# mLSTM, retention and SSD units: a chunk's final transposes share a step with the scores of the chunk three further on

## The chip, the cores and the metric

The kernel runs on one core of one Trainium2 chip. The metric is the device time of one launch in microseconds (us), lower is better; it is given as a median of runs. Every step of the argument is read from one profiled execution. Engines are named as the profile names them: PE (TensorE), PEld (its weight loads), DVE (VectorE), ACT (ScalarE), POOL (GpSimd), SP (DMA issue).

## The reference, cut to what matters

One inference step of a two-layer encoder. A projection W_in is split among four branches, each a causal recurrence done chunk by chunk; the gated results are concatenated and go through W_out. The change touches three branches:

```python
hn = rmsnorm(x, norm_w)
proj = jnp.einsum("btd,dc->btc", hn, w_in)
...
# mLSTM, retention, SSD, each per chunk: scores, output, state
s = jnp.einsum("bhlk,bhsk->bhls", q, k) * dec
o = (jnp.einsum("bhls,bhsv->bhlv", s, v)
     + jnp.exp((idx[None] + 1.0) * lg[:, None])[..., None] * jnp.einsum("bhlk,bhkv->bhlv", q, s_prev))
s_new = jnp.exp(l * lg)[:, None, None] * s_prev + jnp.einsum("bhsk,bhsv->bhkv", kw, v)
...
out_r = head_layernorm(from_blocks(hr)).reshape(bsz, t, GROUP_WIDTH) * jax.nn.silu(rg)
...
y = x + jnp.einsum("btc,cd->btd", jnp.concatenate([out_m, out_r, out_s, out_h], axis=-1), w_out)
```

The prompt has 1024 frames; eight running streams bring 16 frames each.

## The kernel before

The 1152 frames are nine chunks of 128 (eight of the prompt, the ninth the eight streams). Each layer has ten units, two mLSTM (`m`), two retention (`r`), two SSD (`s`) and four HGRN2 (`h`), in the order h r s m h r s m h h. A unit has a projection (its columns of W_in, float32 split into high and low parts: L404 to L406 and L425 to L427, three matmuls for each tile of the contraction) and a mix (the recurrence).

A unit's mix is issued while the next unit's projection runs: r's mix beside s's projection, s's beside m's, m's beside h's. `merge` interleaves the two. A mix is a generator that yields after each step and names its number of steps; after each half of a projection tile `merge` takes as many steps as keep the two in proportion (`j * np_ * pace < i * nm_`, with `nm_` the number of steps). An `after(lag, fn)` puts work off by that many steps. SSD's projection also carries a convolution on DVE (the taps at L1176, the clamp of a SiLU at L526, its sigmoids on ACT at L215, the transposes of its tail on PE at L1200, a product on POOL), tied to projection tiles, not to mix steps. The weights' split into `hi` (ACT, L202) and `lo` (DVE or POOL, L212) is tied to projection tiles too.

A chunk of a mix is made of these parts:

- Z: what the scores need ahead (r: two transposes at L1014 and their copies; m: a copy by head on POOL; s: E prepares the decay).
- A: the scores (r: L1027; m: L812 and L813; s: L1255 and L1258) and their product with the decay on DVE.
- B: the output and the new state (r: L1042, L1043, L1050; m: L841 onwards; s: L1289 onwards). In r, DVE then adds the chunk's product to the state `rS` (L212), scales it (L1059), takes means and variances of the output tile `po` (L1080, L1081), waits for ACT's reciprocal root (L215), normalises (L1085, the last to read `po`) and multiplies by the gate (L212).
- C: two transposes of the gated result on PE (r: L1095, m: L912, s: L1350), a copy out of PSUM, and after two chunks a DMA to `mixd`.

All PSUM tiles (`w` in the trace) come from one pool of eight buffers, whatever asks for them; a projection tile and the parts of a mix draw from it in program order:

```python
self.p_tr = pool("tr", 8, space=PSUM)
```

The step order of r was

```python
A(c); Z(c + 2); yield
B(c - 1); yield
Cc(c - 2); yield
```

and those of m and s the same three steps with E(c + 1) ahead of C. In s, the copies after A and the state update after B were put off with `after(LAG, ...)`.

Of the kernel before, what the change touches and what calls it, by code (L numbers as in the profile page):

```python
# [35 lines left out]
LAG = 1  # L36
# [12 lines left out]
NCH = 9  # L49
# [71 lines left out]
class Kernel:  # L121
    def __init__(self, nc, tc, ctx, T):
        self.nc, self.tc, self.T = nc, tc, T
        pool = lambda name, bufs, **k: ctx.enter_context(tc.tile_pool(name=name, bufs=bufs, **k))
        self.p_const = pool("const", 1)
        self.p_big = pool("big", 6)
        self.p_hi = pool("whi", 2)
        self.p_lo = pool("wlo", 2)
        self.p_raw = pool("wraw", 4)
        self.p_f = pool("f", 18)  # L130
        self.p_c = pool("c", 21)
        self.p_t = pool("t", 8)
        self.p_lay = pool("lay", 1)
        self.p_st = pool("st", 1)
        self.p_s = pool("s", 6)
        self.p_bl = pool("bl", 7)
        self.p_dram = pool("dram", 1, space=DRAM)
        self.p_tr = pool("tr", 8, space=PSUM)
        self.n = 0
        self.ticks = 0  # L140
        self.queue = []
        self.steps = 0
        self.after_queue = []
        self.rest = ((), 0)
# [566 lines left out]
    def unit_m(self, l, p):  # L711
# [38 lines left out]
        def mix():  # L750
# [9 lines left out]
            def Z(c):  # L760
                g, o = divmod(c * 128, G3)
                qz[c] = self.by_head(q[g][:, o:o + 128])
# [167 lines left out]
            use_wi(0)  # L930
            E(0)
            yield
            for c in range(NCH + 1):
                if c % 2 == 0 and c // 2 + 1 < 5:
                    load_e(c // 2 + 1)
                if c % 3 == W1 and c // 3 + 1 < 3:
                    load_wi(c // 3 + 1)
                if c % 3 == W2 and c // 3 + 1 < 3:
                    use_wi(c // 3 + 1)
                if c == 5:  # L940
                    load_states()
                if c < NCH:
                    A(c)
                    if c + 1 < NCH:
                        Z(c + 1)
                    yield
                if c >= 1:
                    B(c - 1)
                    yield
                if c + 1 < NCH:  # L950
                    E(c + 1)
                if c >= 2:
                    Cc(c - 2)
                    yield
            yield
            Cc(NCH - 1)
            yield

        return dict(runs=[("tm", ev_v), ("tm", ev_o), ("tm", ev_z), ("fm", ev_qk)], mix=mix, steps=29, gate=None)


    def unit_r(self, l, p):
# [35 lines left out]
        def mix():  # L998
# [10 lines left out]
            def Z(c):  # L1009

                j, i = divmod(c, 2)
                tr = self.ps("tr")
                for a in range(2):
                    nc.tensor.transpose(tr[:, 128 * a:128 * a + 128], qk[j][:, 256 * i + 128 * a:256 * i + 128 * a + 128], self.ident)  # L1014
                t = self.f()
                self.tt(t[:, 0:256].rearrange("p (h t) -> p h t", h=2), tr[:, None, 0:128].to_broadcast([128, 2, 128]),
                        self.HM[:, :, None].to_broadcast([128, 2, 128]), ALU.mult)
                self.copy(t[:, 256:384], tr[:, 128:256], "a")
                qkT[c] = t
                if c == 8:  # L1020
                    U["zq"] = [self.zq(t[:, 128 * h:128 * h + 128], slice(64 * h, 64 * h + 64)) for h in range(2)]
                    U["km"] = self.km(qk[j][:, 256 * i + 128:256 * i + 256], "c")
# [84 lines left out]
            for c in range(NCH + 1):  # L1107
                if c == 5:
                    load_states()
                if c < NCH:  # L1110
                    A(c)
                    if c + 2 < NCH:
                        Z(c + 2)
                    yield
                if c >= 1:
                    B(c - 1)
                    yield
                if c >= 2:
                    Cc(c - 2)
                    yield  # L1120
            Cc(NCH - 1)
            yield

        return dict(runs=[("tm", ev_qk), ("tm", ev_v), ("tm", ev_g)], mix=mix, steps=29, gate=None)


    def unit_s(self, l, u):
# [96 lines left out]
        def mix():  # L1224
# [26 lines left out]
            def A(c):  # L1251
                g, o = divmod(c * 128, G3)
                cs = slice(o, o + 128)
                sc = self.ps("sc")
                nc.tensor.matmul(sc[:, 0:128], post[2, g][:, cs], post[3, g][:, cs], start=True, stop=True)  # L1255
                tr = sc[:, 128:512]
                for a in range(3):
                    nc.tensor.transpose(tr[:, 128 * a:128 * a + 128], post[a, g][:, cs], self.ident)  # L1258
                e = eb.pop(c)
                Pt[c] = e  # L1260
                xx = self.c(512)
                x, cb_b = self.t(256), self.t(256)
                cb, b_ = cb_b[:, 0:128], cb_b[:, 128:256]
                xd[c], xw[c], xs[c], bt[c] = xx[:, 0:256], xx[:, 256:512], x, b_

                def evac():
                    self.tt(cb, sc[:, 0:128], self.U[c == 8], ALU.mult)
                    self.tt(v4(xx[:, 0:256]), v4(tr[:, 0:256]), sc4(0, c), ALU.mult)
                    self.copy(x, tr[:, 0:256], "a")
                    self.copy(b_, tr[:, 256:384], "a")  # L1270
                    self.tt(e, cb[:, None, :].to_broadcast([128, 4, 128]), e, ALU.mult, "p")
                    self.tt(v4(xx[:, 256:512]), v4(xx[:, 0:256]), sc4(3, c), ALU.mult, "p")
                    self.tt(v4(x), v4(x), self.dsk[:, l, 4 * u:4 * u + 4][:, :, None].to_broadcast([128, 4, 64]), ALU.mult, "p")
                    if c == 8:
                        U["zq"] = self.zq(post[3, g][:, cs])
                        U["km"] = self.km(b_, "c")

                self.after(LAG, evac)

            def B(c):  # L1280
                j, i = divmod(c, 2)
# [13 lines left out]
                if c < 8:  # L1295
                    tr = self.ps("tr")
                    nc.tensor.matmul(tr[:, 0:256], b_, w_, start=True, stop=True)

                    def update():
                        if c == 0:  # L1300
                            self.copy(H, tr[:, 0:256], "v")
                        else:
                            self.tt(v4(H), v4(H), sc4(4, c), ALU.mult)
                            self.tt(H, H, tr[:, 0:256], ALU.add)
                        if c == 7:
                            self.dma(T["o_p_s"][l, 4 * u:4 * u + 4].rearrange("h k v -> k h v"), v4(H))

                    self.after(LAG, update)
                else:
                    km = U.pop("km")  # L1310
                    for jj in range(4):
                        tr = self.ps("tr")
                        for n in range(2):
                            nn = 2 * jj + n
                            nc.tensor.matmul(tr[:, 256 * n:256 * n + 256], km[nn], w_, start=True, stop=True)
                        s = stt[jj]
                        for n in range(2):
                            d = self.sg[:, 5, 8 * (2 * jj + n) + 4 * u:8 * (2 * jj + n) + 4 * u + 4][:, :, None].to_broadcast([128, 4, 64])
                            self.tt(s[:, n], s[:, n], d, ALU.mult, "p")
                        s2 = s.rearrange("p n h e -> p (n h e)")  # L1320
                        self.tt(s2, s2, tr, ALU.add)
                        for n in range(2):
                            self.dma(T["o_s_s"][l, 2 * jj + n, 4 * u:4 * u + 4].rearrange("h k v -> k h v"), s[:, n])
# [48 lines left out]
            for c in range(NCH + 1):  # L1372
                if c + 2 < NCH:
                    load_e(c + 2)
                if c == 5:
                    load_states()
                if c < NCH:
                    A(c)
                    yield
                if c == 0:  # L1380
                    yield
                if c >= 1:
                    B(c - 1)
                    yield
                if c + 1 < NCH:
                    E(c + 1)
                if c >= 2:
                    Cc(c - 2)
                    yield
            yield  # L1390
            yield
            Cc(NCH - 1)
            yield

        return dict(runs=[("fm", ev_x), ("tm", ev_z), ("fm", ev_bc)], mix=mix, steps=33, gate=None)


    def unit_h(self, l, h):
# [602 lines left out]
```

## Time and profile before

| what | before |
|---|---|
| median of 3 runs | 2383.02 us (2382.79 to 2383.59) |
| profiled execution | 2383.27 us |
| its span | 2381.4 us |
| mean granted clock of PE | 0.994 of full |

The span is what the profile covers; 1.9 us of the execution's time lie around it. The profile gives for each engine its busy time, for each stretch of time what was busy in it, and for each wait of an engine which other engine ended it.

### The profile page before, as it was taken

The page shows a single profiled execution, that of the slowest core. Times are in us where ns is not written, and L with a number is a line of the kernel's source. Part 1 is how long each engine was busy: PE and PEld are TensorE (multiplying, and loading weights), DVE is VectorE, ACT ScalarE, POOL GpSimd, SP SyncE. Part 2 cuts the span into 40 slices and gives each one's busy share as a digit, 9 for nine tenths or more (in the row PEclk, how much of TensorE's full clock was granted, in tenths as well). Part 3 has the DMA queues.
Part 4 walks back from the last instruction along what each step waited for, and adds up shares of the span by engine and source line. Part 5 has one row for each costly group of instructions (what it writes and reads, how often), then busy time and mean ns, then how long its engine had stood idle before and what let it go on. Part 6 is the DMA issues. An engine that isn't in the chain of part 4 may idle for free.

```text
span 2381.4 us, 51682 instructions
## 1 busy us (share of the span) xinstructions
PE 2315.6 (97%) x20104; PEld 2251.8 (95%) x20104; DVE 1367.5 (57%) x3426; ACT 1082.4 (45%) x2881; POOL 935.8 (39%) x1117
## 2 busy tenths in 40 slices
PE   7999999999999998999999999999999999899998
PEld 7899999999999998999998999999899999888998
DVE  4756753774765377553258476537747555766532
ACT  6344563433555345424354445634344653453333
POOL 2442344353334335434316333433633452344341
PEclk9999999999999999999999999999999999999999
DMA  5111232221123222546411212322111323225462
GB/s 153 37 47 53 79 90 78 66 61 53 50 84 96 62 73 66 171 126 207 136 49 34 62 55 85 87 70 74 49 54 52 105 72 83 50 86 163 146 189 96
DMA packets 280048, 205.24 MB, mean 86 GB/s; under 512 B 56788, under 2 KB 272236, under 8 KB 279804
## 3 DMA queue, kind: packets, MB, share of 16 engines
q1 hardware_dynamic: 279484, 201.85, 29.9%
q8 instruction: 159, 2.61, 0.5%
q14 instruction: 85, 0.70, 0.1%
q0 software_dynamic: 320, 0.09, 0.0%
HBM read 149.58 MB, written 52.29 MB: 85 GB/s over the span
## 4 chain that ended last, share of the span: by engine, by line
PE 84%; DVE 8%; ACT 4%; DMA 1%; issue 1%; SPq 1%; POOL 1%; ACTq 0%; DVEq 0%; POOLq 0%
PE w L425 16%; PE w L427 16%; PE w L426 16%; PE w L404 6%; PE w L405 6%; PE w L406 6%; DVE f L212 3%; ACT f L215 2%; PE w L1289 1%; DVE c L212 1%; DMA c<-mixd 1%; PE w L1642 1%; PE w L1603 1%; PE w L1552 1%; PE w L1043 1%
## 5 line engine op out<-in xcount | busy, mean ns | idle before, releaser
L425 PE MATMUL w<-hi,hnh 128*128 128x256 f32 (+1 forms) x2592 | 773.3, 298 | 0.0
L427 PE MATMUL w<-hi,hnl 128*128 128x256 f32 (+1 forms) x2592 | 730.1, 282 | 1.6 <-DVE hnl L492 1.4
L426 PE MATMUL w<-lo,hnh 128*128 128x256 f32 (+1 forms) x2592 | 729.3, 281 | 0.0
L425 PEld LDWEIGHTS w<-hi,hnh 128*128 128x128 f32 x2592 | 490.6, 189 | 5.7 <-issue 0.8
L426 PEld LDWEIGHTS w<-lo,hnh 128*128 128x128 f32 x2592 | 490.9, 189 | 2.9
L427 PEld LDWEIGHTS w<-hi,hnl 128*128 128x128 f32 x2592 | 490.3, 189 | 2.2 <-DVE hnl L492 2.0
L215 ACT ACTIVATE f<-f 128x384 f32<-128x384 f32 (+1 forms) x460 | 236.3, 516 | 427.7 <-DVE f L212 263.5
L215 ACT ACTIVATE c<-c 128x512 f32<-128x512 f32 (+3 forms) x398 | 211.3, 534 | 286.3 <-DVE c L526 202.2
L212 POOL TENSOR_TENSOR f<-f,f 128x384 f32<-128x384 f32 (+2 forms) x268 | 225.6, 849 | 290.7 <-ACT f L215 216.3
L404 PE MATMUL w<-hnh,hi 128*128 128x384 f32 x960 | 338.8, 353 | 0.0
L425 PE MATMUL w<-hi,mxh 128*128 128x256 f32 x1152 | 329.4, 286 | 0.0
L427 PE MATMUL w<-hi,mxl 128*128 128x256 f32 x1152 | 325.2, 282 | 0.2 <-POOL mxl L212 0.2
L426 PE MATMUL w<-lo,mxh 128*128 128x256 f32 x1152 | 324.9, 282 | 0.0
L406 PE MATMUL w<-hnh,lo 128*128 128x384 f32 x960 | 324.6, 338 | 0.0
L405 PE MATMUL w<-hnl,hi 128*128 128x384 f32 x960 | 324.6, 338 | 0.0
L212 POOL TENSOR_TENSOR lo<-raw,hi 128x512 fp32r<-128x512 f32 x148 | 196.4, 1327 | 304.3 <-ACT hi L202 278.3
L212 POOL TENSOR_TENSOR c<-c,c 128x512 f32<-128x512 f32 (+2 forms) x144 | 160.3, 1122 | 273.3 <-ACT c L215 169.5
L425 PEld LDWEIGHTS w<-hi,mxh 128*128 128x128 f32 x1152 | 219.0, 190 | 1.4 <-issue 0.6
L427 PEld LDWEIGHTS w<-hi,mxl 128*128 128x128 f32 x1152 | 219.0, 190 | 0.8 <-POOL mxl L212 0.8
L426 PEld LDWEIGHTS w<-lo,mxh 128*128 128x128 f32 x1152 | 218.2, 189 | 0.0
L212 DVE TENSOR_TENSOR lo<-raw,hi 128x512 fp32r<-128x512 f32 x140 | 114.8, 820 | 149.9 <-ACT hi L202 149.7
L404 PEld LDWEIGHTS w<-hnh,hi 128*128 128x128 f32 x960 | 181.5, 189 | 3.0 <-issue 1.8
(295 smaller groups left out, 3876.8 us busy)
## 6 DMA issues: line engine op xcount, KB each, us to landing
raw<-in_w_in SPq DMA_DIRECT2D x224, 128.0 KB
raw<-in_w_in SPq DMA_DIRECT2D x112, 256.0 KB
c<-mixd SPq DMA_DIRECT2D x96, 192.0 KB
raw<-in_w_out SPq DMA_DIRECT2D x64, 256.0 KB
mixd<-c SPq DMA_DIRECT2D x48, 256.0 KB
xd<-c SPq DMA_DIRECT2D x48, 256.0 KB
c<-xd SPq DMA_DIRECT2D x48, 256.0 KB
c<-sscr SPq DMA_DIRECT2D x36, 256.0 KB
```

Source lines behind the costliest of these rows:

```text
L212: (self.nc.vector if e == "v" else self.nc.gpsimd).tensor_tensor(out=out, in0=a, in1=b, op=op)
L215: self.nc.scalar.activation(out=out, in_=in_, func=func, scale=scale, bias=bias, **k)
L404: nc.tensor.matmul(o, hi[:, k, ms], xhi[:, k, :], start=(k == 0), stop=False)
L405: nc.tensor.matmul(o, hi[:, k, ms], xlo[:, k, :], start=False, stop=False)
L406: nc.tensor.matmul(o, lo[:, k, ms], xhi[:, k, :], start=False, stop=(k == KT - 1))
L425: nc.tensor.matmul(o, xhi[:, k, ts], hi[:, k, :w], start=(k == 0), stop=False)
L426: nc.tensor.matmul(o, xhi[:, k, ts], lo[:, k, :w], start=False, stop=False)
L427: nc.tensor.matmul(o, xlo[:, k, ts], hi[:, k, :w], start=False, stop=(k == KT - 1))
L1043: nc.tensor.matmul(po[h], w[:, h], v[j][:, i, h], start=(c in (0, 8)), stop=(c < 8))
L1289: nc.tensor.matmul(po[:, 64 * h:64 * h + 64], pt[:, h], x_[:, 64 * h:64 * h + 64], start=True, stop=True)
L1552: nc.tensor.matmul(sc[rs, 16 * c:16 * c + 16].rearrange("p (n t) -> p n t", t=hs), xt, half(xt), start=True, stop=True)
L1603: nc.tensor.matmul(tr[:, cs], W["KT"][:, cs], v[j][:, i, 0], start=True, stop=True)
```

## The change

A chunk's C is no longer a step of its own. C of chunk c - 3 is issued at the end of the step of A of chunk c (before: C of chunk c - 2, a step behind B of chunk c - 1). r keeps B as a second step; m and s put B of chunk c - 1 and E of chunk c + 1 together in a second step. The last three C are steps of their own at the end. The number of steps falls from 29 to 23 (m, r) and from 33 to 26 (s). In m, Z runs two chunks ahead rather than one. In s, `evac` and `update` are issued at once rather than put off. The pool `t` has 10 buffers, before 8.

```diff
-        self.p_t = pool("t", 8)
+        self.p_t = pool("t", 10)
...
             E(0)
             yield
+            Z(1)
             for c in range(NCH + 1):
...
                     A(c)
-                    if c + 1 < NCH:
-                        Z(c + 1)
+                    if c + 2 < NCH:
+                        Z(c + 2)
+                    if c >= 3:
+                        Cc(c - 3)
                     yield
                 if c >= 1:
                     B(c - 1)
-                    yield
                 if c + 1 < NCH:
                     E(c + 1)
-                if c >= 2:
-                    Cc(c - 2)
-                    yield
+                yield
+            Cc(NCH - 3)
+            yield
+            Cc(NCH - 2)
             yield
             Cc(NCH - 1)
             yield
-        return dict(runs=[("tm", ev_v), ("tm", ev_o), ("tm", ev_z), ("fm", ev_qk)], mix=mix, steps=29, gate=None)
+        return dict(runs=[("tm", ev_v), ("tm", ev_o), ("tm", ev_z), ("fm", ev_qk)], mix=mix, steps=23, gate=None)
...
     def unit_r(self, l, p):
                     A(c)
                     if c + 2 < NCH:
                         Z(c + 2)
+                    if c >= 3:
+                        Cc(c - 3)
                     yield
                 if c >= 1:
                     B(c - 1)
                     yield
-                if c >= 2:
-                    Cc(c - 2)
-                    yield
...
     def unit_s(self, l, u):
-                self.after(LAG, evac)
+                evac()
...
-                    self.after(LAG, update)
+                    update()
...
-        return dict(runs=[("fm", ev_x), ("tm", ev_z), ("fm", ev_bc)], mix=mix, steps=33, gate=None)
+        return dict(runs=[("fm", ev_x), ("tm", ev_z), ("fm", ev_bc)], mix=mix, steps=26, gate=None)
```

In the changed file the lines of `unit_r` are three higher: L1030 for L1027, L1017 for L1014, L1045 for L1042, L1062 for L1059, L1083 and L1084 for L1080 and L1081, L1088 for L1085, L1098 for L1095; the taps are L1182, the tail L1206.

First place: PE, in the mix of the first retention unit, about the scores of the sixth chunk (`w334` before, `w332` after; `f301`, `f304` its query and key, `t310` the gated result of the third chunk whose transposes are C). Before, C stands between projection matmuls, right behind a tail transpose of the convolution:

```order
L426 MATMUL w318_2849<-lo6_2437,hnh21_231 128x256
L427 MATMUL w318_2849<-hi6_2436,hnl22_232 128x256
L1200 MATMUL w324_2919<-cst_107,t293_2677 27x128
L1095 MATMUL w326_2929<-cst_107,t310_2778 128x128 x2
L425 MATMUL w318_2849<-hi6_2436,hnh21_231 128x256
L426 MATMUL w318_2849<-lo6_2437,hnh21_231 128x256
```

After, the same transposes of `t310` follow the scores and Z:

```order
L427 MATMUL w329_2954<-hi6_2430,hnl22_232 128x256
L1030 MATMUL w332_2962<-f304_2750 128x256
L1017 MATMUL w334_2966<-cst_107,c156_1442 128x128 x2
L1098 MATMUL w336_2972<-cst_107,t310_2796 128x128 x2
L425 MATMUL w329_2954<-hi6_2430,hnh21_231 128x256
L426 MATMUL w329_2954<-lo6_2431,hnh21_231 128x256
```

C moved behind A and Z; no instruction of PE is gone. Fewer projection matmuls stand between one B and the next: from B with `w307` to B with `w320` 51 before and 45 after, from there to B with `w340` 51 before and 42 after.

Second place: DVE in the same stretch, from the masking of Z's `w316` to the normalisation of the output tile `w320` of chunk 4. Before, the state update of `rS` comes right after the clamp of a SiLU (L526), and the weight split `lo7` after the gate product:

```order
L212 TENSOR_TENSOR f317_2846<-w316_2843,cst_107 128x256
L526 TENSOR_SCALAR f292_2675<-f292_2675 128x384
L212 TENSOR_TENSOR rS249_2394<-rS249_2394,w321_2879 64x128 x2
L1059 TENSOR_SCALAR rS249_2394<-rS249_2394,cst_107 128x128
L1080 BN_STATS s322_2884<-w320_2874 128x6
L1081 BN_AGGR s322_2884<-s322_2884 128x2
L1080 BN_STATS s322_2884<-w320_2874 128x6
L1081 BN_AGGR s322_2884<-s322_2884 128x2
L1085 TENSOR_SCALAR t323_2891<-w320_2874,s322_2884 128x128 x2
L212 TENSOR_TENSOR t323_2891<-t323_2891,c231_2198 128x256
L212 TENSOR_TENSOR lo7_2809<-raw7_1_2493,hi7_2808 128x2x256
```

After, `lo7` and two taps of the convolution stand ahead of the state update:

```order
L212 TENSOR_TENSOR f317_2848<-w316_2845,cst_107 128x256
L526 TENSOR_SCALAR f288_2654<-f288_2654 128x384
L212 TENSOR_TENSOR lo7_2804<-raw7_1_2493,hi7_2803 128x2x256
L1182 SCALAR_TENSOR_TENSOR f297_2717<-c296_2712,vA_134,f297_2717 128x256
L1182 SCALAR_TENSOR_TENSOR f297_2717<-c296_2712,vA_134,f297_2717 128x128
L212 TENSOR_TENSOR rS249_2394<-rS249_2394,w321_2897 64x128 x2
L1062 TENSOR_SCALAR rS249_2394<-rS249_2394,cst_107 128x128
L1083 BN_STATS s322_2902<-w320_2892 128x6
L1084 BN_AGGR s322_2902<-s322_2902 128x2
L1083 BN_STATS s322_2902<-w320_2892 128x6
L1084 BN_AGGR s322_2902<-s322_2902 128x2
L1088 TENSOR_SCALAR t323_2909<-w320_2892,s322_2902 128x128 x2
```

The split moved ahead of the update. It reads `hi7`, which ACT writes behind the three sigmoids of the SiLU whose clamp is the second row. The buffer of `w320`, which L1088 (before: L1085) is the last to read, goes to the product `w341` of the next chunk's B before, and to that B's output `w340` itself now. The same shifts stand in all four retention units.

Third place: ACT there, from the sigmoids of the gate (`c312`) to the reciprocal root of chunk 4 (`s322`):

```order
L215 ACTIVATE c312_2824<-c312_2824 128x512 x2
L202 ACTIVATE f317_2848<-w316_2845 128x128
L202 ACTIVATE c306_2756<-w318_2851 128x2x128
L215 ACTIVATE f319_2862<-f288_2654 128x384
L215 ACTIVATE f319_2862<-f319_2862 128x384 x2
L202 ACTIVATE hi7_2803<-raw7_1_2493 128x2x256
L215 ACTIVATE s322_2902<-s322_2902,eps_112 128x2
```

Before, the reciprocal root `s322` stood ahead of `hi7`; now `hi7` stands ahead, behind the sigmoids `f319`.

## Rows read from the trace of the kernel before
**Rows 1.** The page: busy time of each engine, and the chain that ended last by engine.

```profile
PE 2315.6 (97%) x20104; PEld 2251.8 (95%) x20104; DVE 1367.5 (57%) x3426; ACT 1082.4 (45%) x2881; POOL 935.8 (39%) x1117
...
PE 84%; DVE 8%; ACT 4%; DMA 1%; issue 1%; SPq 1%; POOL 1%; ACTq 0%; DVEq 0%; POOLq 0%
```

**Rows 2.** Waits of PE: line, what it waited for, us in all, times, longest.

```profile
PE w L1584 <- DVE f L212: 12.0, 8, 2.9
...
PE w L871 <- ACT f L202: 1.7, 2, 0.9
```

**Rows 3.** Windows of the first mixes of r, s, m, and h's start.

```profile
core 0: us, PE busy (x) PEld busy (x) DVE busy (x) ACT busy (x) POOL busy (x), PEclk, DMA share, GB/s
193.00:284.00 91.00, 91.00 (x667) 88.81 (x666) 66.60 (x179) 43.43 (x99) 26.05 (x29) 1.00 0.21 57
291.00:377.00 86.00, 86.00 (x708) 84.14 (x707) 49.31 (x104) 55.11 (x149) 42.83 (x54) 1.00 0.35 92
414.00:481.00 67.00, 67.00 (x510) 64.46 (x509) 48.03 (x158) 29.31 (x111) 21.87 (x29) 1.00 0.26 67
...
505.00:517.00 12.00, 10.06 (x111) 9.60 (x112) 10.82 (x22) 3.48 (x8) 6.97 (x9) 0.86 0.17 45
```

**Rows 4.** Timeline of PE about two C of r: start, us, instructions.

```profile
223.59 0.28 PE L427 MATMUL w<-hi,hnl 128*128 128x256 f32 x1
223.71 0.38 PE L1095 MATMUL w<-cst,t 128*128 128x128 f32 x2
...
224.05 0.27 PE L426 MATMUL w<-lo,hnh 128*128 128x256 f32 x1
...
232.14 0.28 PE L427 MATMUL w<-hi,hnl 128*128 128x256 f32 x1
232.26 0.27 PE L1200 MATMUL w<-cst,t 128*27 128x128 f32 x1
232.37 0.38 PE L1095 MATMUL w<-cst,t 128*128 128x128 f32 x2
...
232.71 0.28 PE L426 MATMUL w<-lo,hnh 128*128 128x256 f32 x1
```

**Rows 5.** Timeline of PE: B of chunks 3, 4 and 5 of r.

```profile
220.62 0.38 PE L1042 MATMUL w<-rS,f 128*128 128x128 f32 x2
...
228.81 0.39 PE L1042 MATMUL w<-rS,f 128*128 128x128 f32 x2
...
237.26 0.38 PE L1042 MATMUL w<-rS,f 128*128 128x128 f32 x2
```

**Rows 6.** Timeline of DVE there; in brackets the idle time before and what ended it.

```profile
222.14 0.58 DVE L212 TENSOR_TENSOR rS<-rS,w 64x128 f32<-64x128 f32 x2 [0.51 <-PE w L1050]
...
225.70 1.77 DVE L1176 SCALAR_TENSOR_TENSOR f<-c,vA,f 128x256 f32<-128x256 f32 x2
...
229.97 0.34 DVE L526 TENSOR_SCALAR f<-f 128x384 f32<-128x384 f32 x1
230.33 0.58 DVE L212 TENSOR_TENSOR rS<-rS,w 64x128 f32<-64x128 f32 x2
...
233.12 0.73 DVE L1085 TENSOR_SCALAR t<-w,s 128x128 f32<-128x128 f32 x2 [0.60 <-ACT s L215]
...
234.23 0.69 DVE L212 TENSOR_TENSOR lo<-raw,hi 128x512 fp32r<-128x512 f32 x1
234.83 0.74 DVE L1176 SCALAR_TENSOR_TENSOR f<-c,vA,f 128x256 f32<-128x256 f32 x2
```

**Rows 7.** Timeline of ACT there: sigmoids of a SiLU, the weights' `hi`.

```profile
230.35 1.64 ACT L215 ACTIVATE f<-f 128x384 f32<-128x384 f32 x3
...
233.00 0.62 ACT L202 ACTIVATE hi<-raw 128x512 fp32r<-128x512 f32 x1
```

**Rows 8.** Timeline of POOL there.

```profile
225.48 1.44 POOL L212 TENSOR_TENSOR lo<-raw,hi 128x512 fp32r<-128x512 f32 x1 [1.09 <-ACT hi L202]
...
232.07 1.01 POOL L212 TENSOR_TENSOR f<-f,f 128x384 f32<-128x384 f32 x1 [0.57 <-ACT f L215]
```

**Rows 9.** Window of a chunk of s in which ACT has most.

```profile
341.00:349.50 8.50, 8.50 (x72) 8.40 (x71) 5.08 (x11) 7.45 (x22) 4.92 (x5) 1.00 0.20 55
```

More of the change, by code (lines that the diff above doesn't have):

```diff
@@ L1117, in mix @@
                     yield
-                if c >= 2:
-                    Cc(c - 2)
-                    yield
+            Cc(NCH - 3)
+            yield
+            Cc(NCH - 2)
+            yield
             Cc(NCH - 1)
             yield
-        return dict(runs=[("tm", ev_qk), ("tm", ev_v), ("tm", ev_g)], mix=mix, steps=29, gate=None)
+        return dict(runs=[("tm", ev_qk), ("tm", ev_v), ("tm", ev_g)], mix=mix, steps=23, gate=None)
     def unit_s(self, l, u):
@@ L1378, in mix @@
                     A(c)
-                    yield
-                if c == 0:
+                    if c >= 3:
+                        Cc(c - 3)
                     yield
@@ L1383, in mix @@
                     B(c - 1)
-                    yield
                 if c + 1 < NCH:
                     E(c + 1)
-                if c >= 2:
-                    Cc(c - 2)
-                    yield
+                yield
+            Cc(NCH - 3)
             yield
+            Cc(NCH - 2)
             yield
```

## The prediction

> **What bounds the kernel now.** I read the page's busy times and chain first, then the waits of PE, then windows of each kind of stage, then the timelines of one retention chunk. The page gives PE 2315.6 us of a span of 2381.4 and 84% of the chain [rows 1], so only two things count: instructions that PE no longer executes, and time in which it waits. In the windows of the first r, s and m mixes PE is busy all of the time at full clock (91.00 of 91.00, 86.00 of 86.00, 67.00 of 67.00 us) [rows 3]: no time waits there to be won. PE idles elsewhere, chiefly where an h unit starts: L1584 alone waits 12.0 us for DVE, and the window of the first such start has 10.06 us of PE in 12.00 at a mean clock of 0.86 [rows 2, 3]. Of the stages that the change touches only L871, the stream part of m, waits: 1.7 us in two waits for an ACT copy [rows 2]. What the change can lose is hidden so far: DVE has 66.60 of 91.00 us in r, ACT 55.11 of 86.00 in s, DVE 48.03 of 67.00 in m [rows 3]. These are means; the steps of a mix come closer together now, so the question is where another engine is full for a whole chunk.
>
> **The merged transposes: 0 us.** 72 of the C that stood alone now stand behind A. A lone C costs PE this: from the L427 before it to the L426 after it 0.46 us (223.59 to 224.05), where two matmuls' spacing takes 0.24 (0.12 from that L427 to where C starts), so 0.22 for the two transposes. Behind a tail transpose the same pair of neighbours is 0.57 apart (232.14 to 232.71), that is 0.33 for three, again 0.11 for each [rows 4]. Standing together saves nothing that these rows show; their rounding of 0.01 us for each C, either way, makes a bound of 0.7 us.
>
> **L871: -1.7 us.** In m the third buffer that the stream part fills was last read by an ACT copy issued a moment before; with another order of requests it gets one that DVE emptied earlier. The wait of 1.7 us goes [rows 2]; bounds 0 (another wait takes its place) and -1.7.
>
> **Denser chunks in r: +7.8 us.** From B of chunk 3 to B of chunk 4 it was 228.81 - 220.62 = 8.19 us, to the next 237.26 - 228.81 = 8.45 [rows 5]. The order has 6 and 9 projection matmuls fewer there; at 0.118 us each (0.24 for two, above) B now come at 0, 7.48 and 14.87 us.
>
> DVE doesn't follow. Count from B of chunk 3. The state add starts 1.52 us after B (222.14 against 220.62), and DVE had been idle 0.51 us for it. The next state add starts at 230.33, 9.71 us after that B, with only a wait for the reciprocal root between (one such wait is 0.60 us): DVE was full and just in time, since 228.81 + 1.52 is the same 230.33 [rows 5, 6]. All this work stands between the two adds after the change as well, so the clamp that came before the add still ends at 230.31 - 220.62 = 9.69. But now the weight split `lo7` comes next. It waits for `hi7`, and that for three sigmoids which themselves wait for the clamp: 1.64 + 0.62 us [rows 7], with the 0.04 and 0.06 us from end to start that these engines show it can begin at about 12.05. The split takes 0.60 (234.23 to 234.83), two taps 0.74 [rows 6]: the state add starts at 13.4, its product ready since 7.48 + 1.52 = 9.0. From the add to the end of L1085 it was 233.12 + 0.73 - 230.33 = 3.52 us [rows 6], so `po` of chunk 4 is free at 16.9. B of chunk 5, due at 14.87, takes this very buffer and stands still for about 1.95 us, all of PE's work behind it. (A tail transpose ahead of it takes the buffer of the state product and stops for part of that; it is the same wait.) In the kernel before, B of chunk 5 didn't need it: only the state product did, and L1085 ended at 233.85, 3.4 us ahead of B at 237.26. Four retention units: 4 x 1.95 = 7.8 us.
>
> Bounds. Low: the two taps at 225.70 took 1.77 us where the two at 234.83 took 0.74; if that 1.03 doesn't recur in the new order, a stall of 0.9 is left. At most another 0.4 may go with single instructions that start earlier than added up: 0.5 each, 2 us in all. High: after the stall B and DVE run in step, the next split again stands ahead of a state add behind its sigmoids, and by the same sums the B after next is late by about 0.5: 2.5 each, 10 us.
>
> POOL's split of 225.48 lasts to 226.92 and ends inside the slow tap, 0.29 us before the end of its first half [rows 6, 8]. The Trainium skill, page "SBUF — State Buffer", section "SBUF: two separate sides", says that VectorE and GpSimd share a pair of ports under an exclusive lock, and that a VectorE instruction with two SBUF inputs is blocked until GpSimd's ends; the slow tap agrees. By this rule the 1.03 comes back, since POOL's split still follows `hi`, and `lo7` would be caught by POOL's product behind the sigmoids (1.01 us, with 0.4 left of it as `lo7` starts): 4 x 2.35 = 9.4 us instead of 7.8, and a time of 2390.7. I keep 7.8, which rests on durations alone.
>
> **Denser chunks in s and m: 0 us.** In s the fullest chunk has ACT 7.45 of 8.50 us [rows 9]. The chunks come about 12% closer, 7.5 us, so ACT is just full there, not over, and the gated result has two steps before its C. If it fails by a chunk's missing slack, up to 1 us in each of four units: bound +4. In m DVE's 48.03 of 67.00 leaves room even 12% denser. Z two chunks ahead takes POOL's copy off A's path, where PE didn't wait. The ten buffers of `t`, and `evac` and `update` at once, cost nothing: the same instructions, issued earlier, hidden under a PE that is full.
>
> **Sum.** 2383.27 (the profiled execution: span 2381.4 and 1.9 around it) + 7.8 - 1.7 + 0 + 0 = 2389.4; the median of the runs is 0.25 lower, so 2389.1, say 2389, +0.25%. Its own bounds: +2 - 1.7 - 0.7 gives 2382.6, +10 + 0.7 + 4 gives 2397.7.
>
> **Rivals.**
>
> - *DVE keeps up (0.35).* If `hi7` isn't late, or the clamp comes earlier since other work of DVE moves behind it, the buffer is free before B is due. The chain has 1.95 us to lose. For it: DVE had 24.4 us of 91.00 free in r [rows 3] and starts the chain on time. Against: the free time lies elsewhere, in this chunk DVE waited only 0.60 us. Then only L871 stays: 2383.0 - 1.7 = 2381.3, with up to 0.4 for each r unit 2383.
> - *Faster (0.13).* The mixes end earlier within their stage, so DVE is free sooner for what h's start waits for. L1584's 12.0 us stand in 8 waits [rows 2]; if half of them were m's mix still in DVE's queue, 6 us go and with them 1.7 of L871: 2375.3, which decides from the point where m's last gate products end before h's first clamp. Against: m's mix is through by 481 and h waits at 505, where DVE's 10.82 us of 12.00 [rows 3] are h's own. A smaller case is that L871 and one or two of these waits go: 2378.
> - *The stall repeats (0.05).* DVE and PE stay in step over three or four chunks of r, or s adds its 4 us: 2398 and above.
> - The forecast itself: 0.47.
>
> **How the numbers follow.** A measurement of this kernel tells about 0.2% (4.8 us) from no change. Slower by more: the forecast but for its low end (a stall below 1.6), 0.42, and the last rival, 0.05: 0.47. Within: DVE keeps up, 0.35, and that low end, 0.05: 0.40. Faster by more: 0.13. Eight in ten leave out the last rival and the larger part of the third: from 2379, the smaller faster case, to 2398. The forecast's own range is 2386 to 2394.
>
> **What the profile would show.** The timeline of the first r mix: a PE idle of 1 to 3 us about 15 us after B of chunk 3 at L1206 and L1045, released by DVE (L212 on `rS`, L1088), in all four units and nowhere else in r; PE's waits gain a line of 4 to 10 us. DVE's split should start right after ACT's `hi`, the state add 4 us after its product. L871 should be gone from the waits; C's transposes should still cost 0.22 us. The prediction is wrong if PE is busy 91 of 91 us in r as before (first rival), if the waits at L1584 shrink (second), or if s or m show a wait at L1289 or L1356.

## The result, and the profile after

The changed kernel takes 2407.56 us in the median (2402.67 to 2409.51, 4 runs) against 2382.9 beside it: a ratio of 1.0101, 95% interval 1.0084 to 1.0119. It is slower by 1.0%; 0.25% was forecast, and the time lies above both stated ranges (2386 to 2394, and 2379 to 2398). The profiled execution took 2405.74 us with a span of 2403.8, 22.4 more than before.

First the page of the changed kernel, busy time of each engine:

```profile
PE 2320.8 (97%) x20104; PEld 2251.7 (94%) x20104; DVE 1363.3 (57%) x3426; ACT 1083.9 (45%) x2881; POOL 935.8 (39%) x1117
```

The instructions are as many as before [rows 1]. Of the 22.4 us, 17.2 are idle time of PE (2403.8 - 2320.8 against 2381.4 - 2315.6), and 5.2 are time in which a matmul record still covers PE. The records themselves are not longer: the mean of the commonest form is 299 ns before and 297 after (first and second row), that of the 384-column L404 353 and 350:

```profile
L425 PE MATMUL w<-hi,hnh 128*128 128x256 f32 x2448 | 731.0, 299 | 0.0
...
L425 PE MATMUL w<-hi,hnh 128*128 128x256 f32 x2448 | 726.4, 297 | 0.0
```

Matmul records overlap: one of 256 columns lasts 0.28 us, and the next starts 0.12 us after it [rows 4]. At a stop the last one runs out with nothing beside it, and the first ones behind the stop start further apart. An estimate from the times between the starts of successive matmuls, each form against its median before, puts 4.4 of the 5.2 us next to stops at full clock and 2.5 into stretches in which half of the full clock was granted (1.2 of 2.4 GHz; 30.7 us of them in this execution, 23.9 in the one before); the rest is -1.6.

The changed kernel's waits of PE are these: line, what it waited for, us in all, times, longest:

```profile
PE w L1589 <- DVE f L212: 10.4, 8, 2.4
...
PE w L912 <- DVE t L903: 5.7, 4, 1.4
PE w L404 <- DVE mC L858: 4.9, 4, 1.7
...
PE w L1206 <- DVE rS L212: 3.7, 4, 0.9
...
PE w L1045 <- DVE t L1088: 3.2, 4, 0.8
PE w L1045 <- DVE rS L1062: 2.2, 4, 0.6
...
PE w L1356 <- ACT t L202: 0.9, 5, 0.2
```

New are 9.1 us in r (L1206, L1045), 10.6 us in m (L912, and a projection matmul L404 that waits for m's state update L858), 0.9 in s. L871 is gone, 1.7 us [rows 2]; the h starts change by up to 1.6 us both ways. The windows of the first three mixes, the same ones as in [rows 3] (columns as there):

```profile
193.00:284.00 91.00, 88.72 (x650) 85.99 (x649) 64.00 (x175) 40.59 (x95) 25.21 (x29) 1.00 0.18 51
291.00:377.00 86.00, 85.82 (x705) 83.74 (x704) 53.53 (x116) 56.17 (x150) 43.79 (x57) 1.00 0.35 93
414.00:481.00 67.00, 64.76 (x495) 61.78 (x495) 44.20 (x145) 26.54 (x103) 20.57 (x28) 1.00 0.24 66
```

r loses 2.28 us of PE, m 2.24, s 0.18, all at full clock: in these windows the clock has no part in it. In r and m DVE is less busy than before (64.00 for 66.60 us, 44.20 for 48.03), and still it is what PE waits for.

The chunk of r that the prediction added up, on DVE (bracket: idle before, and what ended it):

```profile
223.84 0.58 DVE L212 TENSOR_TENSOR rS<-rS,w 64x128 f32<-64x128 f32 x2 [1.63 <-PE w L1053]
...
227.06 1.42 DVE L212 TENSOR_TENSOR t<-t,c 128x256 f32<-128x256 f32 x1
...
231.63 0.35 DVE L526 TENSOR_SCALAR f<-f 128x384 f32<-128x384 f32 x1
234.37 1.08 DVE L212 TENSOR_TENSOR lo<-raw,hi 128x512 fp32r<-128x512 f32 x1 [2.40 <-ACT hi L202]
235.37 0.74 DVE L1182 SCALAR_TENSOR_TENSOR f<-c,vA,f 128x256 f32<-128x256 f32 x2
236.03 0.57 DVE L212 TENSOR_TENSOR rS<-rS,w 64x128 f32<-64x128 f32 x2
236.64 0.28 DVE L1062 TENSOR_SCALAR rS<-rS,cst 128x128 f32<-128x128 f32 x1
...
238.45 0.73 DVE L1088 TENSOR_SCALAR t<-w,s 128x128 f32<-128x128 f32 x2 [0.60 <-ACT s L215]
...
251.70 1.80 DVE L212 TENSOR_TENSOR lo<-raw,hi 128x512 fp32r<-128x512 f32 x1 [2.55 <-ACT hi L202]
```

on POOL:

```profile
226.91 1.28 POOL L212 TENSOR_TENSOR lo<-raw,hi 128x512 fp32r<-128x512 f32 x1 [2.60 <-ACT hi L202]
...
233.90 1.00 POOL L212 TENSOR_TENSOR f<-f,f 128x384 f32<-128x384 f32 x1 [0.75 <-ACT f L215]
```

and on PE:

```profile
222.32 0.38 PE L1045 MATMUL w<-rS,f 128*128 128x128 f32 x2
...
229.81 0.38 PE L1045 MATMUL w<-rS,f 128*128 128x128 f32 x2
...
236.75 0.27 PE L1206 MATMUL w<-cst,t 128*27 128x128 f32 x1 [0.93 <-DVE rS L212]
239.24 0.49 PE L1045 MATMUL w<-rS,f 128*128 128x128 f32 x2 [0.79 <-DVE t L1088]
...
254.46 0.46 PE L1045 MATMUL w<-rS,f 128*128 128x128 f32 x2 [0.56 <-DVE rS L1062]
```

Counted from B of chunk 3 at 222.32: the next B comes at 7.49 (forecast 7.48), the clamp ends at 9.66 (9.69), the split starts at 12.05 (12.05), the state add at 13.71 (13.4), L1088 ends at 16.86 (16.9), and B of chunk 5 starts at 16.92 instead of 14.87. The stop at 254.46 has the same shape: again a split that DVE had to wait for (2.55 us, for ACT's `hi`) stands ahead of the state update.

The split took 1.08 us, not 0.69, with POOL's product behind the sigmoids (233.90 to 234.90) beside it. The gate product at 227.06 took 1.42 us, not 0.43, beside POOL's split (226.91 to 228.19), and the taps behind it 0.73: the 1.03 us that the prediction's low bound was about came back, at another instruction. The Trainium skill, page "SBUF — State Buffer", section "SBUF: two separate sides", has it that a DVE instruction with two SBUF inputs is blocked until a GpSimd instruction that reads SBUF and started first has ended. The trace agrees at both places.

That L1088 ends 0.04 us from the forecast is partly luck. The split cost 0.4 us more than the sum had, and L1062 behind it 0.34 us less, 0.28 for the 0.62 that L1059 took before:

```profile
230.95 0.62 DVE L1059 TENSOR_SCALAR rS<-rS,cst 128x128 f32<-128x128 f32 x1
```

What the prediction didn't have is the end of m's mix. DVE and then PE of the changed kernel there (L1420 to L1453 belong to the next unit's projection, h; L858 is the state update of m's last prompt chunk; L903 writes a gated output, at 478.72 that of this chunk, at 466.33 that of the chunk before it):

```profile
466.33 0.61 DVE L903 SCALAR_TENSOR_TENSOR t<-w,s,c 128x128 f32<-128x128 f32 x2
...
468.82 0.55 DVE L526 TENSOR_SCALAR f<-w 128x384 f32<-128x384 f32 x1
471.07 0.62 DVE L1420 SCALAR_TENSOR_TENSOR f<-f,oml,f 128x384 f32<-128x384 f32 x1 [1.71 <-ACT f L215]
...
474.58 0.36 DVE L1453 TENSOR_SCALAR f<-t 128x384 f32<-128x384 f32 x1
474.86 0.72 DVE L858 SCALAR_TENSOR_TENSOR mC<-mC,s,w 64x129 f32<-64x129 f32 x2
...
478.72 0.61 DVE L903 SCALAR_TENSOR_TENSOR t<-w,s,c 128x128 f32<-128x128 f32 x2
```

```profile
467.56 0.60 PE L851 MATMUL w<-c,t 128*128 128x258 f32 x2
...
475.73 0.41 PE L404 MATMUL w<-hnh,hi 128*128 128x384 f32 x1 [0.83 <-DVE mC L858]
...
479.48 0.41 PE L912 MATMUL w<-cst,t 128*128 128x128 f32 x2 [1.41 <-DVE t L903]
```

The product that L858 adds is ready at 468.2, but a whole chain of h (with a weight split in it), from 468.82 to 474.9 with a wait for ACT, stands ahead of it on DVE. Both stops are waits for a PSUM buffer of this chunk. The projection tile that PE asks for next takes the buffer of its product, which L858 reads last. The C at 479.48 is that of the chunk before, whose gated output was ready at 466.94; what it waits for is the place to write to, the buffer of the last prompt chunk's output tile, which the L903 at 478.72 reads last (by the program's names `w698` takes the buffer of `w682`). In the kernel before that buffer went to a later request, the C of this chunk itself.

There the chain stood ahead of L858 as well. From DVE and PE of the kernel before:

```profile
468.99 0.36 DVE L1448 TENSOR_SCALAR f<-t 128x384 f32<-128x384 f32 x1
469.38 0.73 DVE L858 SCALAR_TENSOR_TENSOR mC<-mC,s,w 64x129 f32<-64x129 f32 x2
...
465.36 0.60 PE L851 MATMUL w<-c,t 128*128 128x258 f32 x2
```

The product was ready at 465.96 and L858 began at 469.38: the lateness was there, about 3.4 us, and hidden. Now it is 6.7 us.

### The profile page after: what moved, and what is told of

It is laid out like the page before. It is cut to its first block, busy times and chain, and to the rows that moved or that the text cites. A ratio compares the mean times of both kernels' runs of the same rounds, so it can differ in the third digit from the quotient of the medians.

```text
span 2403.8 us, 51667 instructions
## 1 busy us (share of the span) xinstructions
PE 2320.8 (97%) x20104; PEld 2251.7 (94%) x20104; DVE 1363.3 (57%) x3426; ACT 1083.9 (45%) x2881; POOL 935.8 (39%) x1117
## 5 line engine op out<-in xcount | busy, mean ns | idle before, releaser
L404 PE MATMUL w<-hnh,hi 128*128 128x384 f32 x960 | 336.0, 350 | 4.9 <-DVE mC L858 4.9
L212 DVE TENSOR_TENSOR lo<-raw,hi 128x512 fp32r<-128x512 f32 x140 | 120.3, 859 | 163.6 <-ACT hi L202 163.4
L404 PEld LDWEIGHTS w<-hnh,hi 128*128 128x128 f32 x960 | 181.4, 189 | 8.7 <-issue 5.6
```

Source lines behind the costliest of these rows:

```text
L212: (self.nc.vector if e == "v" else self.nc.gpsimd).tensor_tensor(out=out, in0=a, in1=b, op=op)
L404: nc.tensor.matmul(o, hi[:, k, ms], xhi[:, k, :], start=(k == 0), stop=False)
```

## The experiments

Theory: merging C costs nothing; the loss comes of chunks that stand closer, at places where DVE, in order, has another stage's work ahead of a chunk's state update. Main rival: the longer lag of C and the other order of requests to the ring of eight PSUM buffers cost, at any spacing. All ratios are against the kernel before, run beside it.

**e1: retention alone.** Edit: `unit_r` of the change, and the ten buffers of `t`, in the kernel before.

> Retention alone is changed, mLSTM and SSD stay as before. Theory (an engine is late for a chunk because chunks stand closer, each place by itself): 2394 us, 11 us over before; PE waits about 9 us at L1206 and L1045 in the four r mixes, none in m at L912 or for L858; L871 keeps its 1.7 us. Rival (the r waits alone are what the prediction added up and the rest comes from the three units together): 2391 and fewer than 8 us of waits.

2400.97 us, ratio 1.008 (1.0064 to 1.0095). The waits in r are those of the full change, to 0.1 us:

```profile
PE w L1203 <- DVE rS L212: 3.8, 4, 1.0
PE w L1042 <- DVE t L1085: 3.2, 4, 0.8
PE w L1292 <- POOL c L212: 3.1, 8, 0.5
PE w L1042 <- DVE rS L1059: 2.1, 4, 0.5
```

So r loses by itself. The time is 7 us over what I expected: s, unchanged here, now waits 3.1 us for POOL at the start of its B, which neither kernel did. The trace tells where that comes from. The last split of DVE beside r starts at 285.37 (280.80 before), after 3.08 us of waiting for ACT's `hi`; the rest of the convolution on DVE and POOL's products behind it move with it, and the one that the first B of s needs starts at 300.49 instead of 295.90, 4.6 us later. That B itself is due only 2.5 us later, and the 1.9 us that it had to spare before don't cover the difference. Why `hi` is late there was not followed up.

**e2: mLSTM alone.** Edit: `unit_m` of the change, and the ten buffers, in the kernel before.

> mLSTM alone is changed. Theory: the last chunks of m lose by themselves, 10.6 us of waits at L912 (for L903) and at a projection matmul (for L858) and about 1 us of refilling, less the 2.5 us that L871 costs now: 2392 us. Rival (m's tail is late only because r and s before it were delayed or left work in the queues): 2382, waits below 2 us.

2394.02 us, 1.005 (1.0035 to 1.0065), with the same 5.7 us at L912 and 4.9 us for L858. m's tail is late by itself.

**e3: merged, but at the old spacing.** Edit, here for r (m and s likewise, with 29 and 33 steps):

```diff
                 if c >= 1:
                     B(c - 1)
                     yield
+                if c >= 2 and c < NCH:
+                    yield
             Cc(NCH - 3)
-            yield
             Cc(NCH - 2)
...
-        return dict(... steps=23, ...)
+        return dict(... steps=29, ...)
```

> The changed kernel with its merged transposes three chunks behind, its earlier Z, evac and update, but with an empty step per chunk again and the old numbers of steps, so that chunks stand as far apart as before. Theory (the spacing costs, merging is free): 2381 to 2383 us, no waits at L1045, L1206, L912. Rival (the longer lag and the other order of PSUM requests cost): 2395 or more, with the same waits.

2384.48 us, 1.0009 (1.0 to 1.0019): none of the new waits is left, L871's is gone. All else of the change is in this kernel, so at the old spacing lag and request order cost nothing that can be told from no change. (One wait at the start of h is longer, 10.6 us at L1580 for 6.9 before; PE's idle time is 66.8 us in all, before 65.8.)

**e4: not merged, but closer.** Edit, in the kernel before:

```diff
-        ... mix=mix, steps=29, ...
+        ... mix=mix, steps=34, ...
-        ... mix=mix, steps=33, ...
+        ... mix=mix, steps=39, ...
```

> The kernel before with its own three steps per chunk, only the numbers of steps that set the pace raised from 29 to 34 (m, r) and 33 to 39 (s), so that chunks come as close as in the changed kernel and nothing is merged. Theory (the spacing costs): 2395 to 2410 us with waits in r and at the end of m. Rival (lag and request order cost): 2383 us, within 3.

2417.74 us, 1.0146 (1.0129 to 1.0163), more than expected; PE waits at other places, in all three units:

```profile
PE w L813 <- POOL t L212: 9.7, 4, 2.4
PE w L1095 <- DVE t L212: 8.5, 4, 2.1
...
PE w L1289 <- POOL c L212: 5.2, 4, 1.3
```

Closer chunks alone make a loss, and a larger one. The lines that wait most here, C of r and the scores of m behind POOL's copy, are those that the change gives more time (C a chunk later, Z a chunk earlier); that this is why they don't wait there is argued, not tried. With e3 the main rival falls as it was put, a cost at any spacing. Not tried is the old request order at the new spacing in the changed kernel. Both stops of m, and the first two of the three in each r, are waits for a buffer, and the order of requests decides who gets a late one; so spacing makes the loss, and the order may have a part in where PE stops.

**e5: no split on DVE beside r.** Edit, in the changed kernel (`beside` is the kind of the unit whose mix runs; lines in its profile and in those of e6, e7, e9 to e11 are one or more higher):

```diff
-        self.tt(lo, raw, hi.bitcast(F32), ALU.subtract, "p" if i in self.gate_cols or q % 2 == 0 else "v")
+        self.tt(lo, raw, hi.bitcast(F32), ALU.subtract, "p" if i in self.gate_cols or q % 2 == 0 or self.beside == "r" else "v")
```

> The changed kernel, but while a retention mix runs the weights' low part is always made by POOL (before: every second one by DVE), so that DVE's state update no longer stands behind the split and the sigmoids that its hi waits for. Theory: by the same chain the clamp ends 9.7 us after B, two taps bring the state add to 10.4 and the free output buffer to 13.9, ahead of the 14.87 at which the next but one B is due; the 9.1 us of waits at L1206 and L1045 go with their refilling, about 11 us: 2396 us, the waits of m stay. Rival (DVE as a whole is too full in r, or POOL's port lock on the taps is what makes it late, and three more splits on POOL make that worse): waits in r of 6 us or more, 2402 to 2412.

2395.35 us, 1.0054 (1.0039 to 1.0069). No wait is left in r; those of m stay:

```profile
PE w L405 <- DVE mC L859: 5.1, 4, 1.7
PE w L913 <- DVE t L904: 4.1, 4, 1.4
```

So r's stall was the splits on DVE, with the sigmoids that their `hi` waits for, ahead of a state update. The edit takes all of them off DVE, six beside the first r (not three, as I had counted), so it doesn't tell their place from their load. The trace does: DVE stood idle for 2.40 and 2.55 us ahead of the two splits shown above, so it was not too full as a whole.

**e6 and e7: h's decay later.** Edit, in the changed kernel (e6), and together with e5's (e7):

```diff
+            chain = lambda: decay(g, x, s, kk, lb, oml)
+            if self.beside == "m" and g < 2:
+                self.later(2, chain)
+            else:
+                chain()
+        def decay(g, x, s, kk, lb, oml):
             nc.vector.scalar_tensor_tensor(out=kk, in0=kk, scalar=oml, in1=s, op0=ALU.mult, op1=ALU.mult)
```

> The changed kernel, but while an m mix runs the DVE part of the h projection's decay (scans and what follows the clamp and exponentials) is put off by one half tile for the first two column groups, so that m's last state update (L858) and gated result (L903) no longer stand behind it. Theory: the 5.7 us at L912 and the 4.9 us at a projection matmul go, with their refilling 11 to 12 us: 2395 us, r's 9 us stay; the start of h, which the third group sets, stays. Rival (those waits come from DVE being late since the chunks before): more than 6 us of them stay, 2401 or more.

> The changed kernel with both of these edits. Theory: only SSD's 0.9 us of waits and the loss around them (2 us) remain against 2.5 us saved at L871: 2382 to 2386 us, same as before. Rival (something else of the denser chunks costs): 2390 or more.

e6: 2409.97 us, 1.0117 (1.0101 to 1.0132); e7: 2401.53 us, 1.0076 (1.0061 to 1.0091). The waits at L912 and for L858 are gone in both, as the theory says; the time is not. In e6, at the start of h:

```profile
PE w L1577 <- POOL f L213: 21.4, 6, 8.1
```

In the changed kernel that line (L1569 there) waited 7.5 us. What was put off on DVE came back as a later start of h. My theory of m was only half right: order decides where the wait shows. That the work of m's last chunks and of h's chains has to go through DVE before h starts, so that no order wins, is argued; the same putting-off at the old spacing, which would tell it from a plain cost of the delay, was not tried.

**e8: SSD alone.** Edit: `unit_s` of the change, and the ten buffers, in the kernel before.

> SSD alone is changed. Theory: 0.9 us of waits at C (L1350's place) and the loss around them, 2 us: 2384 to 2385, no measurable difference. Rival (in SSD too a state update or a gate comes late): 2388 or more.

2384.8 us, 1.0008 (0.9998 to 1.0017). 0.7 us of waits at C; no difference that can be told.

**e9 and e10: only the first group's decay later.** Edit: `g < 2` becomes `g == 0`; e9 with e5's edit, e10 in the kernel before with `unit_m` of the change and the ten buffers.

> As the kernel with both edits, but only the first column group's decay is put off, since m's tail falls beside that group alone, and the second group's delay may be what h's start then waits for. Theory: r's, m's and h's extra waits (L1569's place 21.6 us against 7.5) are all gone: 2382 to 2387 us, within 0.2% of before. Rival (any delay of the decay is paid at h's start): PE waits of 15 us or more there again and 2393 or more.

> mLSTM alone is changed (two steps a chunk), r and s as before, and the first group's decay is put off. Theory: m's denser chunks cost nothing once nothing of h stands ahead of their state update, and L871 has no wait: 2380 to 2383 us, same as before or up to 2.5 us faster. Rival: the waits of m's last chunks or of h's start stay, 2390 or more.

e9: 2396.36 us, 1.0054 (1.0041 to 1.0068); e10: 2394.47 us, 1.0044 (1.0032 to 1.0057). The rival held in both: m's waits are gone, but the same start of h waits 17.2 us in e9 and, in e10,

```profile
PE w L1575 <- POOL f L213: 17.7, 6, 6.8
```

against 6.9 us in the kernel before (L1564 there). About 10 us of waits were exchanged for about 10.

**e11: e5 with m at three steps a chunk.** Edit: e5's, and in m an empty step after B as in e3, 29 steps.

> The changed kernel with the split on POOL beside r, and m alone back at three steps a chunk (its C still merged with A three chunks on, 29 steps); r and s keep their two steps. Theory (m loses by its spacing alone, wherever the wait shows): no waits at L912 or for L858, h's start as before (L1564's place 7 to 11 us), 2382 to 2386 us. Rival (the loss of m comes with r and s, which leave less room behind): 2390 or more.

2387.58 us, 1.0014 (1.0005 to 1.0023). No wait at L912 or for L858, the start of h waits 10.4 us at that line. Giving m its old spacing back took off 7.8 us of e5's time (9.5 by the two ratios) without touching DVE's work: the spacing of m's chunks is what m paid for. What is left over before is 1 to 5 us. In the profiled execution it isn't waiting: PE is idle for 65.9 us, in the kernel before for 65.8.

**e12: r's output copied out of PSUM at once.** Edit, in the changed kernel:

```diff
+                if c < 8:
+                    pc = self.t(256)
+                    self.copy(pc, pb[:, 0:256], "a")
+                    po = [pc[:, 0:128], pc[:, 128:256]]
                 sm = self.s(16)
```

> The changed kernel, but in r ACT copies the output tile of chunks 1 to 8 from PSUM at once, and means, variances and normalisation read the copy, so that the PSUM buffer no longer waits for L1088; the order of DVE is untouched and ACT has 32 copies of about 0.37 us more. Theory (two buffers of the ring make the stall): the 3.2 us at L1045 for L1088 go, the 3.7 us at L1206 for the state add stay, about 2403 to 2405 us. Rival (the state rS itself is late for B): the waits at L1045 stay, now for L1062, and the time is 2407.

2418.08 us, 1.0145 (1.0129 to 1.016): both expectations missed the time. Of their signs, the waits for L1088 went, as the theory had it, and waits at L1045 for L1062 stayed, as the rival had it.

```profile
PE w L1045 <- DVE rS L1062: 8.4, 4, 2.1
...
PE w L1053 <- DVE t L205: 6.1, 4, 1.5
```

The waits for L1088 and for the state add at the tail transpose are gone, but PE stops further on in the same B, at L1053, for a buffer whose reader (a copy of the convolution's tail) stands behind the normalisation on DVE too; and in the next chunk DVE waits 2.84 us for ACT's copy behind sigmoids, and the state is later still. One buffer was not the matter: all that DVE reads at that point is late together.

## Why the prediction was wrong, step by step

- *What bounds the kernel*: right. No instruction of PE is gone, and nearly all of the loss is waits of PE on DVE and what comes with them (0.9 us are waits for ACT, some 2.5 us stand at the lower clock).
- *Merged transposes, 0 us*: right (e3).
- *L871, -1.7 us*: right, the wait is gone.
- *r, +7.8 us*: the mechanism was right to the instruction, and the times of its steps to 0.3 us (the end partly by luck, as above). The size was too small. The sum's own steps give 16.9 - 14.87 = 2.03 for the first stop, not 1.95, and B of chunk 5 did come 2.05 late; the second stop, 0.55, I had worked out (0.5) but left to the upper bound. In idle time that is 1.72 + 0.55 for each unit, 9.1 us; without the splits (e5) the time is 11 to 12 us lower. The lock of the shared ports, which the Trainium skill states (page "SBUF — State Buffer", section "SBUF: two separate sides"), was right about the split; it moved the state add, not the verdict.
- *s, 0 us*: right within the measurement (e8); the 0.9 us of waits at L1356 are one of the signs of being wrong that the prediction named, and too small to tell in the time.
- *m, 0 us*: this step failed. "In m DVE's 48.03 of 67.00 leaves room even 12% denser" took the mean of a stage for its fullest chunks, which is what I had warned of above it. m's last chunks fall beside the h projection's decay chains, and the trace before shows L858 already 3.4 us late there; I looked into r's chunks one by one and not into m's tail. It cost 10.6 us of idle time (e2: 11 us of the whole by itself; e11: 8 to 10 of e5's time).
- *A wait costs its idle time*: a term that was left out. PE's busy time grew by 5.2 us, most of it next to the stops, where matmuls no longer overlap; idle time of 17.2 us went with 22.4 us of span.
- Sum: 7.8 - 1.7 was forecast; 9.1 + 10.6 + 0.9 - 1.7 and some 5 around the waits were measured; the rest are small shifts at h. Alone the parts cost 18 us (r, e1), 11 (m, e2) and 2 (s, e8), together 31, more than the 24.7 of the whole; r alone has the waits of s that the whole change does not have.
- *Rivals*: "the stall repeats", 0.05 at 2398 and above, came nearest in time, though by another place. Its chance was too small, since any unseen place of the same kind adds to it. (Where the prediction says what its eight in ten leave out, "the third" stands for the second rival, the faster one.)

Open: why ACT's `hi` is late at the end of r in e1; whether the old request order at the new spacing would stop PE elsewhere; and whether m could run closer at all, since what was tried moved its wait to h.

## What to carry to other kernels

When steps of a pipeline are brought closer, PE's work is the same, and what counts is how late each state update and each last reader of a PSUM buffer already is: look at every chunk beside every neighbour, the tails above all, not at the busy share of a stage. A chain of in-order sums from rows of the old trace was good to 0.3 us here; the error is in the places it isn't made for. A wait for a buffer is named after its last reader: look which chunk's tile that is before taking it for a wait for data. A wait that is reordered away may come back at the start of the next stage, as in e6, e7, e9 and e10; compare the whole time, not the wait.

## What the runs showed of the hardware

- A wait of PE costs more than its idle time: 17.2 us of added idle time went with 5.2 us of added busy time at the same number of instructions, by the estimate above 4.4 of it next to the stops at full clock; the first pair of matmul records of a B took 0.49 us after a stop (239.24) and 0.38 without one (229.81).
- DVE's split of 0.69 us took 1.08, and the gate product of 0.43 us took 1.42 (227.06), where POOL's instructions with SBUF operands ran beside them; both came back in the same places in all four units of r (1.07 to 1.08 and 1.42 to 1.43 us).
